# The low part of a mixer's weight: a negated copy on ScalarE and an adding transfer instead of a subtraction

## The chip, the core and the metric

The kernel runs on one core of a Trainium2 chip. The core has a matrix engine (TensorE, "PE" in the profile, its weight loads "PEld"), a vector engine (VectorE, "DVE"), an engine for activations and scaled copies (ScalarE, "ACT"), a general engine (GpSimd, "POOL") and SyncE ("SP"), which here issues transfers. Each engine has one queue of instructions and works it off in order; semaphores hold an instruction until what it needs is done. Sixteen DMA engines carry the transfers. The metric is the time of one execution in microseconds on the device; the median of several is what counts.

## What is computed

Two layers of a diffusion backbone work on 256 context and 256 latent tokens of 1024 channels. A layer normalises the tokens, multiplies them by one wide weight `w_in`, gives the products to three token mixers and a gate, merges the branches, and then runs a gated MLP:

```python
u_a, u_b, u_c, u_g = split_cols(h @ p['w_in'], [A_COLS, B_COLS, C_COLS, G_COLS])
...
y_a, y_ac = rwkv7_branch(u_a, u_ac, p)          # A: recurrence over the tokens, both directions
y_b, y_bc = rglru_branch(u_b, u_bc, p)          # B: gated linear recurrence
y_c, y_cc = na_branch(u_c, u_cc, p, update_ctx) # C: neighbourhood attention
x = x + g1 * rms_norm(merge_branches(u_g, y_a, y_b, y_c, p), ng[1])
h = rms_norm(x, ng[2]) * (1.0 + sc2) + sh2
x = x + g2 * rms_norm(conv_ffn(h, p), ng[3])
```

`w_in` has 11520 columns, 90 tiles of 1024 x 128 in each of the two layers. After the last layer only the latent tokens are wanted, so in the second layer gates, queries and some others are computed for 256 columns instead of 512.

## The kernel before

All large products run in float32r, a form of float32 to which a copy rounds. To keep the precision, each operand x is split into a high part hi (x rounded to float32r) and a low part lo = x - hi, and three products are summed: high weight by high tokens (line 246), high weight by low tokens (line 247), low weight by high tokens (line 248). A tile of a weight, 128 partitions by up to 1024 values, takes 8 times these three products.

`wload` (line 217) brings in one tile: SyncE issues the load of the raw tile `wr` (three places in the pool `wp`), ScalarE copies it into `wh` with rounding (line 225), and VectorE or GpSimd subtracts and writes `wl` (line 228). `wh` and `wl` have two places each in `wp`. So a tile's high and low part can be made when the products of the tile before last are done with theirs, while the tile before runs on TensorE. Which engine subtracts is read from the table `CFG[layer]['lo']`: a list for each phase of the layer, 0 for VectorE and 1 for GpSimd. The phases that matter here all load tiles of `w_in`: `st` (start of a layer), `1` (key, value and receptance of the next head pair), `X`, `Y` (recurrence B), `Q` (attention's query, key, value), `G` and `N` (gates). `proj` (line 252) is what they call.

The mixers go over eight head pairs. For a pair, the parts of mixer A's recurrence (line 720 the products r, 735 sa, 741 sp, each followed by an operation of ScalarE, VectorE or GpSimd on the state) alternate on TensorE with projections of B, C, the gates and the next pair. A triangular inverse of each pair's chunks runs on VectorE as some 30 pairs of short operations (lines 664 and 666). A scheduler sets the order on every engine when the kernel is built: it takes instructions by the priorities in `CFG` and by its own estimates of when each could start, so a change of one operation moves others. At run time the order is fixed.

Of the kernel before, what the change touches and what calls it, by code (L numbers as in the profile page):

```python
# [44 lines left out]
for _n, _c in _CS:  # L45
# [6 lines left out]
# per layer: the order in which a head pair's parts are traced, their priorities, how the products of the other  # L52
# mixers are spread beside them, and which engine takes the work that several could take
# [5 lines left out]
  'lo': {'1': [0, 0, 0],  # L59
         'G': [1],  # L60
         'N': [0],
         'Q': [0, 0, 0],
         'X': [0],
         'Y': [0],
# [5 lines left out]
         'st': [1],  # L70
# [38 lines left out]
  'lo': {'1': [0, 0, 0],  # L109
         'G': [1],  # L110
         'N': [0],
         'Q': [0, 1, 0],
         'X': [0],
         'Y': [1],
# [5 lines left out]
         'st': [0],  # L120
# [37 lines left out]
class Net:  # L158
# [51 lines left out]
    # ---- weights: raw -> (hi, lo) in float32r  # L210
    def phase(self, l, name, wps=None):
        """From here on the weights rotate among wps; where their low parts are worked out: 1 for GpSimd."""
        self.lo, self.wn = CFG[l]["lo"][name], 0
        if wps:
            self.wps, self.wi = wps, 0

    def wload(self, ap, kt):
# [8 lines left out]
        eng = nc.gpsimd if self.lo[self.wn % len(self.lo)] else nc.vector  # L226
        self.wn += 1
        eng.tensor_tensor(lo, raw, hi.bitcast(F32), op=ALU.subtract)  # L228
# [36 lines left out]
    # ---- rms statistics of the tokens a ... b - 1: acc holds the sums of squares over the channel tiles  # L265
# [15 lines left out]
    def stat(self, st, sq, a, b, first, last):  # L281
        """Adds the sums of sq over its channels to st, a column for 128 tokens."""
# [13 lines left out]
    # ---- conditioning vectors of a layer: mod[128, 48, 2]  # L296
# [16 lines left out]
    def ada_chunk(self, l, n, kind="c"):  # L313
        """Columns 512 n ... 512 n + 511 of the modulation, four column groups side by side on TensorE."""
# [22 lines left out]
        # modulation: h = x rstd (ng (1 + sc)) + sh ; x += (g ng) o rstd  # L337
# [12 lines left out]
    def layer_consts(self, l):  # L350
# [19 lines left out]
        # softplus(-lam) = max(-lam, 0) + log1p(exp(-|lam|)); log1p(u) = 2 atanh(u / (2 + u))  # L370
# [53 lines left out]
    # ---- A: RWKV-7  # L424
# [16 lines left out]
    def rw_start(self, Q):  # L441
# [4 lines left out]
        # stacked over the partitions: (hi, lo) of w, (lo, hi) of a  # L446
# [14 lines left out]
    def rw_key(self, R, Q, p, n0):  # L461
# [15 lines left out]
        # normalised key  # L477
# [93 lines left out]
    def rw_gram(self, R, u, n0):  # L571
        nc = self.nc
        KR, BK = u["KR"], u["BK"]
        G = R.tile([P, 2, 2, 2, NCH, 64], F32, tag="Gm", name="Gm")  # part, d, h, c
# [22 lines left out]
    def rw_rows(self, R, u, n0):  # L597
# [3 lines left out]
        # from here on [beta; k] decayed to the end of its chunk  # L601
# [3 lines left out]
        # value rows by token, for both directions  # L605
# [12 lines left out]
        # rows by token of [beta; k]  # L618
# [13 lines left out]
    def rw_inv(self, R, u):  # L632
# [9 lines left out]
        if self.cfg['f1']:  # L642
            # the block beside them makes room for the rows of keys
# [10 lines left out]
        # columns s of the inverse: rows 0-63 hold the odd ones, rows 64-127 the even ones, both in the even places  # L654
# [16 lines left out]
    def rw_inv2(self, R, u):  # L671
# [4 lines left out]
        T1 = Ap  # rows 0-31: T11, rows 96-127: Q  # L676
# [134 lines left out]
    # ---- B: RG-LRU  # L811
# [16 lines left out]
    def lru_gates(self, B, u, d):  # L828
# [4 lines left out]
        if self.cfg['lq']:  # L833
            # the parts of the products lie where the second direction's values come
# [54 lines left out]
    # ---- C: neighbourhood attention  # L889
    def softmax(self, C, ps, nk):  # L890
        """ps: list of PSUM views [128, nk] (same width); returns normalised probabilities in SBUF."""
# [22 lines left out]
    def attn_qkv(self, C, p, n0):  # L914
# [13 lines left out]
        # values: 4 windows of 4 rows by 32 columns, then the context  # L928
# [8 lines left out]
    def attn_pre(self, C, u, n0):  # L937
        nc = self.nc
        q, k, vw = u["q"], u["k"], u["vw"]
        # queries by blocks (n, r, c): rotated, then plain  # L940
# [8 lines left out]
        if self.cfg['sq']:  # L949
            # (hi, lo) of a head's plain queries over the partitions, the high parts in the head's own half; the  # L950
            # high parts of the context's keys in both halves, the low ones beside each other
# [489 lines left out]


class _Off:
    """Columns n0 ... 511 of the 512 tokens, addressed by their place among the 512."""

    def __init__(self, ap, n0):
        self.ap, self.n0 = ap, n0
# [147 lines left out]
```

## Time and profile before

| what | value |
|---|---|
| median of three runs | 3066.45 us |
| the three runs | 3055.29, 3066.45, 3069.74 us |
| span of the profiled execution, first to last instruction | 3050.6 us |
| TensorE busy in the span | 2886.2 us |
| VectorE busy | 1968.9 us |
| ScalarE busy | 1411.1 us |
| GpSimd busy | 840.6 us |
| mean granted clock of TensorE | 0.959 |

The profile's own execution is known by its span alone, which lies 16 us under the median of the runs and 5 us under the fastest; sums below are differences to that span and are then put on the median. The mixers of the first layer lie between about 30 and 1100 us, those of the second between 1790 and 2692 us; merging, output product and MLP fill the rest. A product's busy time is longer than the distance to the next one's start, as products are pipelined; distances between starts are the better price of a product.

### The profile page before, as it was taken

To read this page: it belongs to the slowest core of one execution; us is meant where nothing else is said; L and a number is where in the kernel's file an instruction comes from. 1 tells how busy PE (TensorE), PEld (TensorE's weight loads), DVE (VectorE), ACT (ScalarE), POOL (GpSimd) and SP (SyncE) were. 2 spreads that over 40 slices of the span, in tenths; PEclk is the share of its full clock that TensorE was granted. 3 is DMA by queue.
4 is the path that set the end of the run, shared out by engine and by line. 5 is a ranking of instruction groups with operands and counts; after the bars stand their busy time and mean duration, and the time that the engine had idled before them with its cause. 6 is when DMAs were issued, how large, how long until landed. Compare 5 with 4: busy or idle time off the path is not lost. (4 is left out here: it accounts for less than half of the span.)

```text
span 3050.6 us, 53179 instructions
## 1 busy us (share of the span) xinstructions
PE 2886.2 (95%) x21104; PEld 2265.9 (74%) x21104; DVE 1968.9 (65%) x3745; ACT 1411.1 (46%) x2485; POOL 840.6 (28%) x788
## 2 busy tenths in 40 slices
PE   7999999999999999999999998998999999998998
PEld 5666776766767678687778886776776777788898
DVE  6757658576686653465444267788677778775784
ACT  4454455554455452253323245454554545554553
POOL 3341322424234225100000113433432433414220
PEclk9999999999999899998999998998988999999899
DMA  6222122211222225755562352222222122245653
GB/s 229 81 70 67 59 71 66 74 60 56 69 76 70 84 100 180 273 190 180 198 223 92 107 183 82 62 78 69 68 72 69 62 70 78 77 140 205 222 188 115
DMA packets 130553, 344.39 MB, mean 113 GB/s; under 512 B 14720, under 2 KB 41600, under 8 KB 130304
## 3 DMA queue, kind: packets, MB, share of 16 engines
q1 hardware_dynamic: 123392, 334.69, 33.1%
q10 hardware_dynamic: 6912, 6.29, 0.7%
q8 instruction: 166, 2.72, 0.4%
q14 instruction: 83, 0.68, 0.1%
HBM read 301.08 MB, written 25.17 MB: 107 GB/s over the span
## 5 line engine op out<-in xcount | busy, mean ns | idle before, releaser
L225 ACT ACTIVATE wh<-wr 128x1024 fp32r<-128x1024 f32 (+1 forms) x402 | 420.8, 1048 | 581.0 <-PE pj L247 209.1
L248 PE MATMUL pj<-hh,wl 128*128 128x512 f32 (+1 forms) x1440 | 559.0, 389 | 41.4 <-DVE wl L228 40.0
L246 PE MATMUL pj<-hh,wh 128*128 128x512 f32 (+1 forms) x1440 | 569.7, 397 | 5.8 <-ACT gt L1088 3.0
L228 DVE TENSOR_TENSOR wl<-wr,wh 128x1024 fp32r<-128x1024 f32 (+1 forms) x310 | 398.2, 1285 | 266.5 <-ACT wh L225 244.2
L247 PE MATMUL pj<-hl,wh 128*128 128x512 f32 (+1 forms) x1440 | 556.0, 386 | 0.0
L228 POOL TENSOR_TENSOR wl<-wr,wh 128x1024 fp32r<-128x1024 f32 (+1 forms) x92 | 221.1, 2403 | 637.1 <-ACT wh L225 343.6
L248 PEld LDWEIGHTS pj<-hh,wl 128*128 128x128 f32 x1440 | 280.7, 195 | 104.6 <-DVE wl L228 45.7
L246 PEld LDWEIGHTS pj<-hh,wh 128*128 128x128 f32 x1440 | 280.6, 195 | 70.0 <-issue 16.4
L247 PEld LDWEIGHTS pj<-hl,wh 128*128 128x128 f32 x1440 | 280.4, 195 | 55.1 <-issue 13.4
L666 DVE TENSOR_TENSOR AT<-AT,itmp 128x126 f32<-128x126 f32 (+22 forms) x496 | 154.7, 312 | 11.8
L732 POOL TENSOR_TENSOR r<-SV,gC 64x256 f32<-64x256 f32 x96 | 84.2, 877 | 242.0 <-DVE SV L745 139.8
L664 DVE TENSOR_TENSOR itmp<-AT 128x126 f32<-128x126 f32 (+22 forms) x496 | 138.1, 278 | 12.0
L585 PEld LDWEIGHTS gram<-KR,BK 64*128 64x128 f32 x1024 | 116.3, 193 | 27.4 <-ACT Gm L590 14.8
L585 PE MATMUL gram<-KR,BK 64*128 64x128 f32 (+1 forms) x1024 | 131.3, 288 | 4.9 <-ACT Gm L590 4.7
L246 PE MATMUL fo<-fh,wh 128*128 128x256 f32 (+1 forms) x418 | 131.0, 313 | 0.0
L248 PE MATMUL fo<-fh,wl 128*128 128x256 f32 (+1 forms) x418 | 130.7, 313 | 0.0
L247 PE MATMUL fo<-fl,wh 128*128 128x256 f32 (+1 forms) x418 | 130.4, 312 | 0.0
L246 PE MATMUL fu<-hh,wh 128*128 128x256 f32 (+1 forms) x384 | 126.2, 330 | 3.1 <-DVE fgs L1347 2.4
L246 PE MATMUL fg<-hh,wh 128*128 128x256 f32 (+1 forms) x384 | 127.2, 333 | 0.1
L248 PE MATMUL fu<-hh,wl 128*128 128x256 f32 (+1 forms) x384 | 126.4, 330 | 0.8 <-DVE wl L228 0.8
L247 PE MATMUL fg<-hl,wh 128*128 128x256 f32 (+1 forms) x384 | 126.0, 330 | 0.0
L247 PE MATMUL fu<-hl,wh 128*128 128x256 f32 (+1 forms) x384 | 125.8, 328 | 0.0
(344 smaller groups left out, 6481.6 us busy)
## 6 DMA issues: line engine op xcount, KB each, us to landing
wr<-in_w_in SPq DMA_DIRECT2D x180, 512.0 KB, 3.2
aw<-in_ada_w SPq DMA_DIRECT2D x96, 512.0 KB, 4.4
wr<-in_ffn_w_in SPq DMA_DIRECT2D x96, 512.0 KB, 3.4
wr<-in_w_branch SPq DMA_DIRECT2D x48, 512.0 KB, 3.3
wr<-in_ffn_w_out SPq DMA_DIRECT2D x36, 512.0 KB, 3.5
wr<-in_w_out SPq DMA_DIRECT2D x24, 512.0 KB, 4.4
Gm<-KR SPq DMA_DIRECT2D x32, 256.0 KB, 3.6
wr<-in_ffn_w_out SPq DMA_DIRECT2D x18, 384.0 KB, 3.1
```

What stands on the lines that cost most here:

```text
L225: nc.scalar.activation(hi, raw, AF.Copy)
L228: eng.tensor_tensor(lo, raw, hi.bitcast(F32), op=ALU.subtract)
L246: nc.tensor.matmul(o, lhsT=a, rhs=xh[k][:, n0:n1], start=(first and k == 0), stop=False)
L247: nc.tensor.matmul(o, lhsT=a, rhs=xl[k][:, n0:n1], start=False, stop=False)
L248: m = nc.tensor.matmul(o, lhsT=b, rhs=xh[k][:, n0:n1], start=False, stop=(last and k == kt - 1))
L585: nc.tensor.matmul(ps[:, i, 0:nx], lhsT=BK[hs, d, c, :], rhs=KR[hs, 0:nx, d, c, :], start=True, stop=True)
L664: eng.tensor_tensor(tmp, Ap[:, q + 1:32, q:q + 1].to_broadcast([P, nt, ns]), Tf[:, q:q + 1, 0:2 * ns:2].to_broadcast([P, nt, ns]), op=ALU. ...
L666: eng.tensor_tensor(Tf[:, q + 1:32, 0:2 * ns:2], Tf[:, q + 1:32, 0:2 * ns:2], tmp, op=ALU.subtract)
L732: nc.gpsimd.tensor_tensor(sg, S0, gcb, op=ALU.mult)
```

## The change

In the phases `st`, `1`, `X`, `Y`, `Q`, `G` and `N` of both layers the table now holds 2. For these tiles no engine subtracts. ScalarE reads the raw tile a second time and writes it, rounded as the high part is, with the opposite sign into the low part's place; then GpSimd issues a transfer that reads the whole weight from DRAM once more and adds it to what stands there, so that x - hi remains. The tables of the other phases (`m0`, `m1`, `wo`, `fi`, `fo`, `fp`) stay, and the table of the second layer changes like the first's. Comments are dropped elsewhere in the file, and line numbers behind the edit grow by 5.

```diff
-  'lo': {'1': [0, 0, 0],
-         'G': [1],
-         'N': [0],
-         'Q': [0, 0, 0],
-         'X': [0],
-         'Y': [0],
+  'lo': {'1': [2],
+         'G': [2],
+         'N': [2],
+         'Q': [2],
+         'X': [2],
+         'Y': [2],
...
-         'st': [1],
+         'st': [2],
...
         nc.scalar.activation(hi, raw, AF.Copy)
-        eng = nc.gpsimd if self.lo[self.wn % len(self.lo)] else nc.vector
+        how = self.lo[self.wn % len(self.lo)]
         self.wn += 1
-        eng.tensor_tensor(lo, raw, hi.bitcast(F32), op=ALU.subtract)
+        if how == 2:
+
+            nc.scalar.activation(lo, raw, AF.Copy, scale=-1.0)
+            nc.gpsimd.dma_start(lo, ap, accum_op=ALU.add)
+        else:
+            (nc.gpsimd if how else nc.vector).tensor_tensor(lo, raw, hi.bitcast(F32), op=ALU.subtract)
```

The scheduler's order moves with it. 174 of the 402 tiles take the new way; VectorE has 177 subtractions of weights instead of 310, GpSimd 51 instead of 92, ScalarE 174 copies more, and GpSimd 174 transfers where it had none.

On TensorE, in the second layer where the key tile of a head pair (`pj11`) begins, the order before was this (`pj60` is the tile before, `lr` and `li` belong to mixer B, `pj36` is a tile of 256 columns, `wl_19601` and `wl_19730` are low parts):

```order
L248 MATMUL pj60_19597<-hh7_15574,wl_19601 128x512
L846 MATMUL lr_19633<-xb_19394,gw_19361 128x512
L847 MATMUL li_19634<-xb_19394,gw_19361 128x512
L246 MATMUL pj36_19646<-hh0_15567,wh_19649 128x256
L246 MATMUL pj11_19726<-hh0_15567,wh_19729 128x512
L247 MATMUL pj11_19726<-hl0_15575,wh_19729 128x512
L248 MATMUL pj11_19726<-hh0_15567,wl_19730 128x512
L246 MATMUL pj11_19726<-hh1_15568,wh_19729 128x512
```

And the same place in the changed kernel (`pj36` now stands as a whole between `pj60` and `pj11`, whose low part is `wl_19852`; `avt` are transposes of attention's values):

```order
L251 MATMUL pj36_19767<-hh7_15664,wh_19770 128x256
L252 MATMUL pj36_19767<-hl7_15672,wh_19770 128x256
L253 MATMUL pj36_19767<-hh7_15664,wl_19771 128x256
L987 MATMUL avt_19828<-cst_86,vw_19650 128x128 x4
L251 MATMUL pj11_19848<-hh0_15657,wh_19851 128x512
L252 MATMUL pj11_19848<-hl0_15665,wh_19851 128x512
L251 MATMUL pj19_19884<-hh0_15657,wh_19887 128x512
L253 MATMUL pj11_19848<-hh0_15657,wl_19852 128x512
```

The key tile's low part takes the place that `pj60` had; between the last product of `pj60` and the first low product of `pj11` there stand now the 24 products of `pj36`, four transposes and three products.

On VectorE, near the end of the inverse (`AT`, `itmp`) of that head pair, before:

```order
L664 TENSOR_TENSOR itmp_19342<-AT_19260 128x78
L666 TENSOR_TENSOR AT_19260<-AT_19260,itmp_19342 128x6x13
L664 TENSOR_TENSOR itmp_19345<-AT_19260 128x70
L666 TENSOR_TENSOR AT_19260<-AT_19260,itmp_19345 128x5x14
L228 TENSOR_TENSOR wl_19730<-wr_19727,wh_19729 128x1024
L664 TENSOR_TENSOR itmp_19348<-AT_19260 128x56
L666 TENSOR_TENSOR AT_19260<-AT_19260,itmp_19348 128x4x14
```

and in the changed kernel (`ib` and `z` belong to mixer B):

```order
L669 TENSOR_TENSOR itmp_19458<-AT_19376 128x78
L671 TENSOR_TENSOR AT_19376<-AT_19376,itmp_19458 128x6x13
L669 TENSOR_TENSOR itmp_19461<-AT_19376 128x70
L876 TENSOR_TENSOR ib_19518<-ib_19518,z_19517 128x1024
L671 TENSOR_TENSOR AT_19376<-AT_19376,itmp_19461 128x5x14
L878 SCALAR_TENSOR_TENSOR z_19517<-av_19516,ib_19518 128x512
L669 TENSOR_TENSOR itmp_19464<-AT_19376 128x56
```

The subtraction is gone from between the steps of the inverse, and operations of mixer B have moved in.

On GpSimd, at the same key tile, in the changed kernel (`bias` is attention's position bias, `z` and `sq` belong to mixer B):

```order
L975 TENSOR_TENSOR sw_19817<-sw_19817,cst2_16721 128x256
L231 DMA wl_19721<-in_w_in 128x1024
L231 DMA wl_19771<-in_w_in 128x1024
L924 TENSOR_TENSOR bias_19645<-bias_19645,cst2_16721 128x512
L231 DMA wl_19852<-in_w_in 128x1024
L884 TENSOR_TENSOR z_19517<-z_19517 128x256
L231 DMA wl_19888<-in_w_in 128x1024
```

Each transfer stands in line with the engine's other work, behind `bias` and in front of `z`, and waits there for ScalarE's copy.

## Rows read from the trace of the kernel before

**Rows 1.** The page's first part: busy us, share of the span, instructions of each engine.
```profile
PE 2886.2 (95%) x21104; PEld 2265.9 (74%) x21104; DVE 1968.9 (65%) x3745; ACT 1411.1 (46%) x2485; POOL 840.6 (28%) x788
```

**Rows 2.** Table by stretch, both mixers: engines' busy us (instructions), granted clock, DMA share, GB/s.
```profile
30.00:1100.00 1070.00, 1031.24 (x7204) 738.95 (x7197) 712.45 (x1504) 518.12 (x960) 345.98 (x342) 0.97 0.22 72
1790.00:2692.00 902.00, 840.65 (x6452) 653.03 (x6451) 690.56 (x1345) 466.76 (x841) 323.77 (x339) 0.94 0.24 78
```

**Rows 3.** List of waits, whole span: us in total, times, longest us.
```profile
DVE SV L745 <- PE sp L741: 115.1, 61, 4.5
...
PEld pj L248 <- DVE wl L228: 45.7, 15, 7.8
...
PEld r L720 <- DVE SV L745: 20.7, 26, 2.4
...
PEld sp L741 <- ACT SV L737: 17.1, 45, 0.8
...
PEld gram L585 <- ACT Gm L590: 14.8, 25, 1.9
...
PEld Q L685 <- DVE AT L678: 11.3, 10, 1.8
PEld sa L735 <- ACT r L724: 11.3, 38, 0.8
...
PEld yt L791 <- DVE cen L778: 9.9, 6, 3.2
...
PEld kbc L493 <- ACT th L490: 9.0, 8, 1.9
```

**Rows 4.** Line 228 in the second layer's mixers: who waited for it (us, times).
```profile
  PEld pj L248: 45.7, 15
```

**Rows 5.** Timeline at one such wait: start us, us, engine, work, idle before it.
```profile
2122.57 0.23 DVE L666 TENSOR_TENSOR AT<-AT,itmp 128x70 f32<-128x70 f32 x1
2122.72 1.22 DVE L228 TENSOR_TENSOR wl<-wr,wh 128x1024 fp32r<-128x1024 f32 x1
...
2123.99 0.29 PEld L248 LDWEIGHTS pj<-hh,wl 128*128 128x128 f32 x1 [7.81 <-DVE wl L228]
```

**Rows 6.** Table by stretch behind that wait (columns as in rows 2).
```profile
2124.00:2128.00 4.00, 4.00 (x9) 3.13 (x10) 3.72 (x11) 0.00 (x0) 0.00 (x0) 0.50 0.38 135
```

**Rows 7.** Timeline of TensorE, projections at full clock: starts of following products.
```profile
2237.23 0.39 PE L246 MATMUL pj<-hh,wh 128*128 128x512 f32 x1
2237.45 0.39 PE L247 MATMUL pj<-hl,wh 128*128 128x512 f32 x1
...
2238.02 0.28 PE L248 MATMUL pj<-hh,wl 128*128 128x256 f32 x1
2238.14 0.28 PE L246 MATMUL pj<-hh,wh 128*128 128x256 f32 x1
```

**Rows 8.** The page's groups: count, busy us, mean ns of one, idle before it.
```profile
L225 ACT ACTIVATE wh<-wr 128x1024 fp32r<-128x1024 f32 (+1 forms) x402 | 420.8, 1048 | 581.0 <-PE pj L247 209.1
...
L228 DVE TENSOR_TENSOR wl<-wr,wh 128x1024 fp32r<-128x1024 f32 (+1 forms) x310 | 398.2, 1285 | 266.5 <-ACT wh L225 244.2
...
L228 POOL TENSOR_TENSOR wl<-wr,wh 128x1024 fp32r<-128x1024 f32 (+1 forms) x92 | 221.1, 2403 | 637.1 <-ACT wh L225 343.6
...
L732 POOL TENSOR_TENSOR r<-SV,gC 64x256 f32<-64x256 f32 x96 | 84.2, 877 | 242.0 <-DVE SV L745 139.8
```

**Rows 9.** Timeline: a subtraction on GpSimd, a step of the inverse on VectorE.
```profile
2111.09 2.44 POOL L228 TENSOR_TENSOR wl<-wr,wh 128x1024 fp32r<-128x1024 f32 x1
...
2111.30 2.38 DVE L666 TENSOR_TENSOR AT<-AT,itmp 128x126 f32<-128x126 f32 x1
```

**Rows 10.** The page's DMA parts: a queue's share; an issue's size and us to landing.
```profile
q1 hardware_dynamic: 123392, 334.69, 33.1%
...
wr<-in_w_in SPq DMA_DIRECT2D x180, 512.0 KB, 3.2
```

**Rows 11.** Timeline of SyncE: one issue of a transfer.
```profile
327.65 0.33 SPq L1089 DMA_DIRECT2D gd<-gt  x1
```

More of the change, by code (lines that the diff above doesn't have):

```diff
@@ L108 @@
   'hp': 10000,
[L109 to L114, printed above, removed]
+  'lo': {'1': [2],
+         'G': [2],
+         'N': [2],
+         'Q': [2],
+         'X': [2],
+         'Y': [2],
          'fi': [0, 1, 0],
@@ L119 @@
          'm1': [0],
-         'st': [0],
+         'st': [2],
          'wo': [1]},
```

## The prediction

> **What bounds the kernel now.** I read the page first for the engines' shares: TensorE is busy for 2886 us of a span of 3050.6, 95% [rows 1]. So whatever happens elsewhere counts only where TensorE waits. Then I read the two mixer stretches, which hold all the weights that the change touches: in the first layer TensorE is busy for 1031 of 1070 us, in the second for 841 of 902, while VectorE is at 67% and 77% and ScalarE at 48% and 52% [rows 2]. The list of waits then says what TensorE idles for there. The largest single entry is a projection's third product (line 248) that waits for its weight's low part from VectorE: 45.7 us in 15 waits on the weight-load side [rows 3]. All 45.7 us lie in the second layer's mixers [rows 4].
>
> The timeline shows what one of them is. A product's weight load stands idle for 7.81 us until 2123.99, and VectorE does the subtraction of 1.22 us at 2122.72, behind a long row of steps of 0.2 to 0.3 us of a triangular inverse [rows 5]. VectorE was not short of time for the subtraction, the subtraction stood late in its queue. And TensorE pays again afterwards: the granted clock of the 4 us behind that wait is 0.50, the lower of its two levels [rows 6], which loses another 2 us.
>
> **What the change removes.** 174 of the 402 weights change their way. The order of instructions on VectorE loses 133 subtractions and GpSimd's loses 41. At 1.285 and 2.403 us each [rows 8] that is 171 us of VectorE and 99 us of GpSimd. TensorE sees of it the 45.7 us above: the inverse no longer stands in front of a low part. The other waits of TensorE for VectorE in the list sum to 20.7 + 11.3 + 9.9 = 42 us [rows 3]. VectorE's busy share in the mixers falls from 71% (1403 of 1972 us, [rows 2]) to 62%, so I take an eighth of the 42 off, 5 us; half of it, 21 us, is the most I would believe. GpSimd's subtractions also held VectorE up: a step of the inverse took 2.38 us beside one of them [rows 9], where others take 0.23 [rows 5]. That is VectorE's time off the path and I leave it at nothing.
>
> **What it adds, outside the new chain.** ScalarE gets 174 more copies of the high part's form, 1.048 us each [rows 8]: 182 us, so its share in the mixers goes from 50% to 59%. TensorE's waits for ScalarE in the recurrence and beside it are 17.1 + 11.3 + 14.8 + 9.0 = 52 us [rows 3]; scaled by 59/50 they cost 10 us more. The second reading of 174 weights is 91 MB. At the rate of the load queue (334.69 MB in 33.1% of 3050.6 us, or 331 GB/s, [rows 10]) one takes 1.6 us of all sixteen DMA engines, whose mean share in the mixers is 0.22 to 0.24 [rows 2]: one reading adds 0.14 to that share, two passes 0.28. There is room; cost nothing. The raw tile has three places, so holding it for one more copy costs nothing either; what hides that is that loads are issued a tile ahead.
>
> **The new chain, and what it does to TensorE.** A low part has two places. The place is free when the last low product of the tile before last is done. From then on the changed kernel needs, in a row: the semaphore, 0.1 us; ScalarE's high part, 1.05; the instructions that stand on ScalarE between high and low part, 1.9 on the mean in the new order, at 0.55 each (985 us in 1801 instructions, [rows 2]), 1.1; the negated copy, 1.05; GpSimd's queue, 0.4 (a third of the time busy, with instructions of 0.98 us on the mean, [rows 2]); the issue of the transfer; and its landing. The trace has no transfer issued by GpSimd and none that adds. For the issue the ends are 0.33 us (an issue of SyncE, [rows 11]) and 2.4 (the subtraction that it replaces there, [rows 8]); I take 1.0, nearer to the first, since no data passes through the engine. For the landing the ends are a plain load of the same 512 KB, 3.2 us, and two of them one behind the other, 6.4 [rows 10]; the add must read the destination as well as the weight, so neither end fits, and I take the middle, 4.8. Sum: 0.1 + 1.05 + 1.1 + 1.05 + 0.4 + 1.0 + 4.8 = 9.5 us, against about 2.4 for the two operations of before.
>
> How long may it be? I counted, in the changed kernel's order on TensorE, the work between that release and the first low product of the new tile, each product at the mean distance from start to start that its form has in the trace (at full clock 0.23 us for 512 columns, 0.12 for 256, [rows 7]; the means are longer, as they hold before's waits and its slow clock). For 172 tiles the median span is 12.2 us. 14 spans are under 7 us, 25 under 8, 47 under 9, 59 under 9.5, 72 under 11, 86 under 12. The tight ones are the key tiles of the next head pair, 5 to 7 us in both layers, and in the second layer the 256-column tiles and those behind them. What is missing, summed over the tiles, is 19 us for a chain of 7 us, 38 for 8, 69 for 9, 96 for 9.5, 126 for 10, 192 for 11, 271 for 12. As a check, the same count in the order of before gives 31 us for a chain of 5 and 51 for 6, where the trace has 45.7: so before's chain acted as one of 5.7 us, 3.3 more than its two operations, and the excess was the queue. With that excess instead of my 1.5 us of queues the new chain would be 11.3 us and miss some 215 us; I keep it for the range, as ScalarE and GpSimd have no row of waiting work like VectorE's inverse.
>
> What is queued behind the new waits: on ScalarE the copies of the recurrence, on GpSimd the scaled state of line 732 (96 of them, 0.88 us, [rows 8]), which the next step of the recurrence adds. VectorE takes that only after another product, for which it already waits 115 us [rows 3], so a delay of a microsecond there is covered; a longer one is not.
>
> The load row alone would make the landing 3.2 us, the chain 7.9 and the sum of the next part 3,061 us. The Trainium skill, page Collectives: The Full Stack, section "Why ReduceScatter is half of AllGather", says that an add inside the DMA engines needs two reads for each write and so runs at half the copy's rate; by it, the 1.6 us of moving double and the landing is an estimate of 4.8 us, which gives 3,121. No run here has yet shown which.
>
> **The sum.** +96 (missing in the chain) - 46 (the old wait) + 10 (ScalarE) - 5 (VectorE) = +55 us. The loss of clock behind each wait is on both sides, about 2 us each time, and I let it cancel. On the profiled execution that is a span of 3050.6 + 55 = 3,106 us. The median of the three runs is 3066.45, 16 us above that span (the runs lie between 3055.29 and 3069.74), so the forecast is 3066 + 55 = **3,121 us**.
>
> **Rivals.**
> *The old wait goes and nothing takes its place* (faster). The scheduler has put the tiles further apart than before, and if the chain takes no more than 7 us only 19 us are missing. Time: 3066 + 19 - 46 - 21 = 3,018 us. For it speaks that only 14 spans are under 7 us; against it, that even a plain load leaves 7.9 us by the rows. It decides from a chain below 7.5 us (27 us missing). Chance 0.26, between 2,995 and 3,050.
> *A draw.* The chain is about 8 us, 38 us missing: 3066 + 38 - 46 + 5 = 3,063 us. Chance 0.16.
> *The add is slow or the issue is* (much slower). A landing of 6.4 and an issue of 2.4 make the chain 12.5 us: some 317 us missing, 3066 + 317 - 46 + 5 = 3,342 us. Every second tile would then stop TensorE, evenly in both layers. Chance 0.12 for 3,250 and more.
> *The recurrence pays* (slower). 128 state copies of 0.38 us on ScalarE (line 737) and 96 operations of line 732 on GpSimd now have 174 copies and as many waiting issues between them. If each of the 96 comes a microsecond later than VectorE asks for it, that is 96 us in place of the count above, 3066 + 96 - 46 + 5 = 3,121 us: the forecast's time by another road, with VectorE and not a DMA named behind TensorE's waits. Chance 0.12.
> That the change doesn't do what it says is excluded by the order: 174 transfers on GpSimd, 174 copies on ScalarE, no subtraction of these tiles left.
>
> **How the numbers follow.** Forecast, from 3,082 to 3,250, chance 0.34 by the DMA chain and 0.12 by the recurrence; draw 0.16; faster 0.26; much slower 0.12. A measurement of this kernel can tell about 0.5% from no change, 15 us. Faster 0.26, same 0.16, slower 0.58. The range leaves some tenth out at either end: from 3,025, inside the fast rival, to 3,270, just inside the slow one.
>
> **What would show it.** In the changed kernel's list of waits, "wl from VectorE" should be gone for projections, and in its place a wait of line 253's products for a DMA, some 60 to 120 us in 40 to 70 pieces, longest at the key tiles, in both layers. The DMA part should list 174 transfers of 512 KB at 4 to 6 us to landing. VectorE should fall by about 170 us, ScalarE rise by 180, TensorE's busy time stay. A landing under 3.5 us would make the fast rival true; one above 6 the slow one. If there is no wait for a DMA and the time is still longer, the recurrence's waits on lines 725, 740 and 746 must have grown, and the count of spans was beside the point.

## The result, and the profile after

The changed kernel takes 3312.16 us, the median of four runs (3305.81 to 3319.99), beside 3060.87 us for the kernel before on the same chip (3052.03 to 3069.74). The ratio is 1.0819, 95% interval 1.0782 to 1.0856. The forecast was 3121 us with a range up to 3270: the direction was right and the size was not.

The page's first part, which answers to [rows 1]; the span of this execution is 3306.2 us, that of before 3050.6:

```profile
PE 3008.7 (91%) x21104; PEld 2356.1 (71%) x21104; DVE 1765.3 (53%) x3612; ACT 1571.4 (48%) x2659; POOL 844.8 (26%) x921
```

TensorE does the same 21104 products, but is busy 122.5 us longer and idle for 297.5 us where it was 164.4. These two, 122.5 and 133.1, are the whole 255.6 us of longer span. The table by stretch for the mixers, which answers to [rows 2], shows where the busy time came from. The stretches are cut a little inside the mixers: the last recurrence product `sp` of the first layer now starts at 1217.6 where it was 1092.5, 125 us later, and the second layer's projections now run from 1935 to 2954.

```profile
30.00:1170.00 1140.00, 1028.52 (x6630) 739.89 (x6625) 603.55 (x1384) 564.62 (x991) 346.80 (x396) 0.89 0.43 101
1900.00:2900.00 1000.00, 898.08 (x6429) 700.64 (x6427) 570.23 (x1272) 537.48 (x920) 306.25 (x394) 0.88 0.48 114
```

The granted clock was 0.97 and 0.94 there, and is 0.89 and 0.88. The DMA engines' share doubled, from 0.22 and 0.24 to 0.43 and 0.48. The list of waits (us in total, times, longest), to set beside [rows 3], names what TensorE idles for, and the last two lines who releases the two transfers of a tile:

```profile
PEld pj L253 <- DMA wl<-in_w_in: 191.3, 67, 6.8
PE pj L253 <- DMA wl<-in_w_in: 169.0, 61, 6.1
...
PEld sp L746 <- ACT SV L742: 20.1, 49, 1.0
PEld r L725 <- DVE SV L750: 16.6, 40, 0.8
...
PEld sa L740 <- ACT r L729: 13.7, 44, 0.6
...
PEld gram L590 <- ACT Gm L595: 8.7, 16, 1.2
PEld Q L690 <- DVE AT L683: 7.6, 8, 1.8
...
POOL wl L231 <- ACT wl L230: 495.3, 105, 22.4
...
SPq L222 <- ACT wl L230: 908.7, 128, 17.9
```

The old wait for a subtraction is gone. In its place the same product (now line 253) waits 191.3 us in 67 pieces for the adding transfer. On the side of the products the wait is 169.0 us, where the kernel before had this line:

```profile
PE pj L248 <- DVE wl L228: 40.0, 9, 7.4
```

The 129.0 us between the two are nearly all of the 133.1 us by which TensorE's idle time grew. The other waits of TensorE are near what they were. Groups and DMA issues of the page, to set beside [rows 8] and [rows 10] (group: count, busy us, mean ns; queue: packets, MB, share of 16 engines; issue: count, KB, median us to landing):

```profile
L231 POOL DMA_DIRECT2D wl<-in_w_in x174 | 154.1, 886 | 622.8 <-ACT wl L230 495.3
L233 DVE TENSOR_TENSOR wl<-wr,wh 128x1024 fp32r<-128x1024 f32 (+1 forms) x177 | 226.8, 1282 | 176.6 <-ACT wh L225 175.5
...
q1 hardware_dynamic: 123392, 334.69, 32.2%
q0 software_dynamic: 25056, 91.24, 16.1%
...
wr<-in_w_in SPq DMA_DIRECT2D x180, 512.0 KB, 3.8
wl<-in_w_in POOLq DMA_DIRECT2D x174, 512.0 KB, 7.8
```

The issue on GpSimd takes 0.89 us, and the landing 7.8 us from the start of the issue. The timeline of one tile shows why the two releases belong together: ScalarE's negated copy ends at 331.23, and releases two transfers at once, the raw load of a later tile at 331.26 and this tile's adding transfer at 331.53.

```profile
330.19 1.04 ACT L230 ACTIVATE wl<-wr 128x1024 fp32r<-128x1024 f32 x1
...
331.26 0.33 SPq L222 DMA_DIRECT2D wr<-in_w_in  x1
...
331.53 0.86 POOL L231 DMA_DIRECT2D wl<-in_w_in  x1 [8.06 <-ACT wl L230]
...
339.51 0.19 PEld L253 LDWEIGHTS pj<-hh,wl 128*128 128x128 f32 x1 [3.23 <-DMA wl<-in_w_in]
```

The table by stretch in and behind this wait (columns as in rows 2) shows the DMA engines at a share of 0.64 while TensorE waits, where the whole stretch has 0.43, and then at nothing. It has 11 products in 4 us at a clock of 0.57, mostly the lower of the two levels, 1.2 GHz, and 27 in the next 3.5 us at 1.00, which is 2.4 GHz:

```profile
335.60:339.50 3.90, 0.83 (x11) 0.54 (x10) 1.73 (x3) 3.64 (x5) 0.93 (x1) 1.00 0.64 151
339.50:343.50 4.00, 3.98 (x11) 3.12 (x12) 4.00 (x4) 0.00 (x0) 3.42 (x2) 0.57 0.00 0
343.50:347.00 3.50, 3.50 (x27) 2.71 (x25) 1.43 (x2) 0.82 (x1) 1.42 (x2) 1.00 0.00 0
```

### The profile page after: what moved, and what is told of

Same layout as the page of the kernel before. It is cut to its first block, busy times and chain, and to the rows that moved or that the text cites. A ratio compares the mean times of both kernels' runs of the same rounds, so it can differ in the third digit from the quotient of the medians.

```text
span 3306.2 us, 53463 instructions
## 1 busy us (share of the span) xinstructions
PE 3008.7 (91%) x21104; PEld 2356.1 (71%) x21104; DVE 1765.3 (53%) x3612; ACT 1571.4 (48%) x2659; POOL 844.8 (26%) x921
## 3 DMA queue, kind: packets, MB, share of 16 engines
q0 software_dynamic: 25056, 91.24, 16.1%
## 5 line engine op out<-in xcount | busy, mean ns | idle before, releaser
L253 PE MATMUL pj<-hh,wl 128*128 128x512 f32 (+1 forms) x1440 | 596.4, 415 | 169.5 <-DMA wl<-in_w_in 169.0
L251 PE MATMUL pj<-hh,wh 128*128 128x512 f32 (+1 forms) x1440 | 592.9, 413 | 12.0 <-ACT gt L1093 5.9
L252 PE MATMUL pj<-hl,wh 128*128 128x512 f32 (+1 forms) x1440 | 586.1, 407 | 0.0
L253 PEld LDWEIGHTS pj<-hh,wl 128*128 128x128 f32 x1440 | 299.8, 208 | 247.1 <-DMA wl<-in_w_in 191.3
L251 PEld LDWEIGHTS pj<-hh,wh 128*128 128x128 f32 x1440 | 302.2, 210 | 78.7 <-issue 19.4
L233 DVE TENSOR_TENSOR wl<-wr,wh 128x1024 fp32r<-128x1024 f32 (+1 forms) x177 | 226.8, 1282 | 176.6 <-ACT wh L225 175.5
L231 POOL DMA_DIRECT2D wl<-in_w_in x174 | 154.1, 886 | 622.8 <-ACT wl L230 495.3
L233 POOL TENSOR_TENSOR wl<-wr,wh 128x1024 fp32r<-128x1024 f32 (+1 forms) x51 | 121.4, 2380 | 511.7 <-DVE fgs L1352 287.8
L230 ACT ACTIVATE wl<-wr 128x1024 fp32r<-128x1024 f32 x174 | 182.9, 1051 | 0.4 <-PE pj L253 0.2
L750 DVE TENSOR_TENSOR SV<-sp,r 64x256 f32<-64x256 f32 x96 | 39.8, 415 | 227.6 <-PE sp L746 226.4
L671 DVE TENSOR_TENSOR AT<-AT,itmp 128x126 f32<-128x126 f32 (+22 forms) x496 | 132.4, 267 | 12.8
L729 ACT ACTIVATE r<-r 64x256 f32<-64x256 f32 x128 | 48.6, 380 | 179.5 <-PE r L725 165.0
```

Of the source, the lines that this page charges most:

```text
L230: nc.scalar.activation(lo, raw, AF.Copy, scale=-1.0)
L231: nc.gpsimd.dma_start(lo, ap, accum_op=ALU.add)
L233: (nc.gpsimd if how else nc.vector).tensor_tensor(lo, raw, hi.bitcast(F32), op=ALU.subtract)
L251: nc.tensor.matmul(o, lhsT=a, rhs=xh[k][:, n0:n1], start=(first and k == 0), stop=False)
L252: nc.tensor.matmul(o, lhsT=a, rhs=xl[k][:, n0:n1], start=False, stop=False)
L253: m = nc.tensor.matmul(o, lhsT=b, rhs=xh[k][:, n0:n1], start=False, stop=(last and k == kt - 1))
```

## The experiments

Times are medians; the ratio is to the kernel before, run on the same chip in the same job.

**1. The same transfer without the add.** The order of instructions on all five engines is that of the changed kernel.

```diff
-            nc.gpsimd.dma_start(lo, ap, accum_op=ALU.add)
+            nc.gpsimd.dma_start(lo, ap)
```

> The changed kernel with one thing taken out: GpSimd's transfer writes the weight over the negated copy instead of adding it (so the low part is the whole weight and the result is not the reference's). The order on all five engines is that of the changed kernel. Landing theory (the slowdown is the adding transfer's 7.8 us against two places for low parts, and the half clock behind each wait): without the second read the landing falls by some 1.5 us to about 6.2, TensorE's waits for it from 191 to 100 to 140 us, the time to 3,160 to 3,230 us. Order theory (the slowdown comes from the new order and from the longer queues on ScalarE and GpSimd, whatever the transfer takes): 3,290 us or more.

Measured: 3104.49 us, ratio 1.017 (1.0129 to 1.0211). The page and the list of waits of this run:

```profile
L231 POOL DMA_DIRECT2D wl<-in_w_in x174 | 101.4, 583 | 543.2 <-ACT wl L230 416.6
...
q0 software_dynamic: 25056, 91.24, 8.7%
...
wl<-in_w_in POOLq DMA_DIRECT2D x174, 512.0 KB, 4.5
```

```profile
PEld pj L253 <- DMA wl<-in_w_in: 63.3, 42, 3.9
```

With a landing of 4.5 us in place of 7.8, the excess over the kernel before falls from 251 to 51 us, further than expected. The new order of instructions and the copies and issues in the queues are still there, and cost 51 us at most, so the theory that blamed the order falls. The add doubles the transfers' engine time: 16.1% of 3306.2 us against 8.7% of 3102.8, 532 against 270 us for the same bytes.

**2. Three places for low parts**, paid for with a raw place. This is meant to take the wait for a free place off the chain and to leave the transfer as it is.

```diff
-        raw = pool.tile([P, 1024], F32, tag="wr", name="wr", bufs=3 if pool is self.wp else None)[:, :kt * P]
+        raw = pool.tile([P, 1024], F32, tag="wr", name="wr", bufs=2 if pool is self.wp else None)[:, :kt * P]
...
-        lo = pool.tile([P, 1024], F32R, tag="wl", name="wl")[:, :kt * P]
+        lo = pool.tile([P, 1024], F32R, tag="wl", name="wl", bufs=3 if pool is self.wp else None)[:, :kt * P]
...
-        lw = self.wp.tile([P, 1024], F32, tag="wr", name="lw", bufs=3)[:, :640]
+        lw = self.wp.tile([P, 1024], F32, tag="wr", name="lw", bufs=2)[:, :640]
```

> The changed kernel with three places for low parts instead of two in the weights' pool, paid for with two places for raw weights instead of three. Landing theory: a third place gives each low part one more tile's time, so waits for the transfer fall under 60 us, the granted clock comes back to 0.94 or more, and the time is 3,040 to 3,110 us. Order theory: the same copies and transfers stand in the queues, so 3,230 us or more.

Measured: 3064.4 us, ratio 1.0028 (1.0007 to 1.0048). Nearly everything is regained; 11 us are left. Its list of waits and its DMA part held a surprise:

```profile
PEld pj L253 <- DMA wl<-in_w_in: 49.2, 14, 5.7
...
SPq L222 <- ACT wh L225: 609.0, 114, 16.6
```

```profile
q0 software_dynamic: 25056, 91.24, 17.4%
...
wl<-in_w_in POOLq DMA_DIRECT2D x174, 512.0 KB, 5.5
```

The landing itself fell to 5.5 us, while the transfers' engine time stayed: 17.4% of 3063.9 us are 533 us, where the changed kernel had 532. So in the changed kernel the adding transfer does not take more of the engines, it is spread over a longer time.

With a free place at hand the scheduler puts the negated copy ahead of the high part's in 156 of 174 tiles, and the raw load is then released by the high copy (line 225) and no longer by the negated one. I went through all 174 adding transfers of both traces, and call one accompanied when a raw load is issued between 1 us before and 1.5 us after it. In the changed kernel 145 are, and land after 7.9 us (median). Here 26 are, and land after 7.5, while the 69 with no raw load from 3 us before to 4 us after land after 5.3. The order on ScalarE goes with it within this one run: of the 156 tiles with the negated copy first 10 are accompanied, and the 156 land after 5.4; of the other 18, 16 are, and the 18 land after 7.7. So the landing seems to depend on company; experiment 9 tests this.

The rule is rough: in the changed kernel the 29 that are not accompanied still land after 6.9, nearly all of them beside some other transfer; only 3 of the 174 share no more than 1 us with any, and these land after 5.3 to 5.5.

**3. One layer at a time.** The table of one layer is set back to that of before, so that only the other layer uses the transfer.

> The new way in the first layer's mixers alone, the second layer as before. Landing theory: 92 us of waits and as much again in clock are new there, and before had no wait of this kind to lose: 3,061 plus 120 to 160, so 3,180 to 3,220 us. Order theory: half of the slowdown, about 3,185 us, with waits spread over other lines and no fall of the clock.

> The new way in the second layer's mixers alone, the first layer as before. Landing theory: 93 us of new waits less the 46 us of old ones, and the clock: 3,061 plus 80 to 130, so 3,140 to 3,190 us, and this and the first-layer kernel's excess together make the whole 251 us. Order theory: the same sum, but no smaller than the first layer's half.

Measured: 3188.75 us, ratio 1.0441 (1.0396 to 1.0486), for the first layer alone and 3170.51, ratio 1.0387 (1.0327 to 1.0447), for the second. The excesses of 135 and 117 us sum to 252, the whole. The loss lies in both layers and they do not share it.

**4. The negated copy first.**

```diff
+            nc.scalar.activation(lo, raw, AF.Copy, scale=-1.0)
+            nc.gpsimd.dma_start(lo, ap, accum_op=ALU.add)
             nc.scalar.activation(hi, raw, AF.Copy)
-            nc.scalar.activation(lo, raw, AF.Copy, scale=-1.0)
-            nc.gpsimd.dma_start(lo, ap, accum_op=ALU.add)
```

> The changed kernel with ScalarE's two copies of a weight tile in the other order: the negated copy first and the adding transfer issued behind it, the high part after that. One copy (1.05 us) leaves the chain from a free place to a landed low part, and the adding transfer begins before ScalarE has released the raw tile's place, so its start no longer coincides with the load of a later raw tile. If the waits come from the length of this chain, 1.0 to 2.0 us less of it takes 80 us for each us (the counted spans between a chain of 11 and of 12 us), half as much again for the clock: 3130 to 3240 us, the landing down from 7.8 to 6.0 to 7.5 us. If instead the high part was what TensorE needed first and the delay moves to it, PEld's and PE's waits for the high copy on ScalarE grow by 100 us or more in all and the time stays at 3280 us or above.

Measured: 3245.15 us, ratio 1.0622 (1.0575 to 1.067), just outside the expected 3130 to 3240. The excess over the kernel before falls from 251 to 195 us, but the landing stayed at 7.5 us, and 142 adding transfers are still accompanied by a raw load. The edit did only a part of what it says: in the trace the negated copy runs ahead of the high one in 51 of the 174 tiles, and in the other 123 the scheduler still puts the high copy first. The 51 land after 7.0 us, the 123 after 7.8. So the run does not price a chain without the high copy, and whether a shorter chain and a landing without company come together it leaves open.

**5. The low products last**, in the changed kernel and in the kernel before.

```diff
         for k in range(kt):
-            a, b = hi[:, k * P:(k + 1) * P], lo[:, k * P:(k + 1) * P]
+            a = hi[:, k * P:(k + 1) * P]
             nc.tensor.matmul(o, lhsT=a, rhs=xh[k][:, n0:n1], start=(first and k == 0), stop=False)
-            nc.tensor.matmul(o, lhsT=a, rhs=xl[k][:, n0:n1], start=False, stop=False)
-            m = nc.tensor.matmul(o, lhsT=b, rhs=xh[k][:, n0:n1], start=False, stop=(last and k == kt - 1))
+            m = nc.tensor.matmul(o, lhsT=a, rhs=xl[k][:, n0:n1], start=False, stop=False)
...
+        for k in range(kt):
+            m = nc.tensor.matmul(o, lhsT=lo[:, k * P:(k + 1) * P], rhs=xh[k][:, n0:n1], start=False, stop=(last and k == kt - 1))
```

> The changed kernel with the products of a weight tile in another order: all products with the high part first, then those with the low part (same products, same sum). The low part of a full tile is wanted 14 to 16 products of 0.23 us later, some 3.5 us, while its place comes free as late as before. If the length of the chain against the span between two uses of a place is the cause, this is a chain of 9 us in place of 12.5: 70 to 130 us of waits in place of 360, less lost clock: 3060 to 3140 us. If the waits come from somewhere else (the transfers' total, GpSimd's queue), no wait is shortened and the time stays above 3250 us.

> The kernel before with the same order of products (all with the high part, then all with the low one), subtraction as it was. If the kernel before lost its 46 us of waits for the low part, and the half-clock stretches behind them, to a part that came 1 to 3 us late, these go: 2990 to 3035 us. If the waits for the attention and recurrence operands set the time there, or move into the place of the old ones, 3040 to 3070 us.

Measured: 3146.77 us, ratio 1.0296 (1.0243 to 1.035), with the transfer, and 3195.9, ratio 1.0429 (1.0356 to 1.0503), with the subtraction. The first fits the theory of the span between uses, a little above the expected range: the landing is still 7.7 us, and TensorE's waits for it fall from 191.3 to 85.7 us, with the granted clock at 0.940:

```profile
PEld pj L256 <- DMA wl<-in_w_in: 85.7, 44, 4.4
```

The second was a plain miss. No wait of a projection for its low part is left in its list, and yet the kernel loses 4%. The profile is of the longest of its four executions, 3222.18 us; the other three had a mean granted clock of 0.919 to 0.932, where the kernel before in the same job had 0.952 to 0.964. Their span times the missing clock is 215 to 259 us, where the kernel before had 110 to 147, so most of the loss goes with the lower clock. What lowers the clock there, without those waits, I did not find.

**6. Control: the kernel before with the places of experiment 2.**

> Control for the run of the changed kernel with three places for low parts and two for raw tiles: the kernel before with the same places, subtraction as it was. If the third place is worth as much to the kernel before (its waits of 46 us were for a place that came free late), 3000 to 3035 us. If its waits were for VectorE's queue behind other work, the place takes nothing off, and two raw places cost it some: 3045 to 3090 us.

Measured: 3092.01 us, ratio 1.014 (1.0085 to 1.0196). The two changes of places together cost the subtraction 1.4%, although its waits for low parts fall from 45.7 to 28.7 us; which of the two costs it, this run does not show. With equal places the adding transfer is the faster way, by 1.1%.

```profile
PEld pj L253 <- DVE wl L233: 28.7, 12, 5.1
```

**7. A better third place.** In experiment 2 the second layer's key tiles still waited 3.0 to 3.6 us each on the side of the products. The timeline of one shows a raw place held by the recurrence's small weights (`lw`, loaded at 2122.64): VectorE's last reading of them (line 241) ends at 2128.61, the next raw load follows at 2128.68, and the wait for the low part ends at 2140.13.

```profile
2122.64 0.33 SPq L470 DMA_DIRECT2D lw<-in_lora  x1
...
2125.53 0.63 ACT L238 ACTIVATE lh<-lw 128x512 fp32r<-128x512 f32 x1 [1.97 <-DMA lw<-in_lora]
...
2127.92 0.69 DVE L241 TENSOR_TENSOR ll<-lw,lh 128x512 fp32r<-128x512 f32 x1
...
2128.68 0.33 SPq L222 DMA_DIRECT2D wr<-in_w_in  x1
...
2132.07 1.06 ACT L230 ACTIVATE wl<-wr 128x1024 fp32r<-128x1024 f32 x1 [4.37 <-DMA wr<-in_w_in]
...
2140.13 0.29 PEld L253 LDWEIGHTS pj<-hh,wl 128*128 128x128 f32 x1 [3.82 <-DMA wl<-in_w_in]
```

So the small weights got another place, on top of experiment 2; the second run adds the edit of experiment 4, the third is the subtraction with the same places.

```diff
-        lw = self.wp.tile([P, 1024], F32, tag="wr", name="lw", bufs=2)[:, :640]
-        nc.sync.dma_start(lw, self.ins["lora"][self.l, p])
+        lw = T2("ta")
+        nc.sync.dma_start(lw, self.ins["lora"][self.l, p, :, :512])
...
-        nc.gpsimd.tensor_copy(gw, lw[:, 512:])
+        nc.sync.dma_start(gw, self.ins["lora"][self.l, p, :, 512:])
```

> The changed kernel with three places for low parts and two for raw tiles, as in the run with three places, and with the recurrence's small weights (lora, 640 columns) no longer loaded into a raw place: 512 columns go to a scratch tile of the recurrence (ta), 128 straight into the gate's weights (gw). In the run with three places the second layer's key tiles still waited 3.0 to 3.6 us each, 24 us in all, and there the raw load of the key tile was issued only once the lora tile had left one of the two raw places. If that place was the cause, the 24 us and the half-clock stretches behind them go: 3020 to 3045 us. If two raw places are too few in themselves, or the scratch tile comes free too late, 3050 to 3080 us.

> As the run with the lora weights' own place, and with ScalarE's negated copy ahead of the high part's. The chain is one copy (1.05 us) shorter and the adding transfer starts before the raw place is released. If chain length still costs with three places, 10 to 30 us under that run: 3000 to 3030 us. If the third place has already covered the chain, the same time within 10 us.

> Control: the kernel before (subtraction) with the same places, three low, two raw, and the lora weights in the scratch tile. With three low and two raw places the subtraction ran at 1.014 and the adding transfer at 1.003 of the kernel before, some 30 us apart. If VectorE's and GpSimd's freed time is worth that wherever the landing is covered, this run is 20 to 40 us above the one with the transfer: 3045 to 3080 us. If those 30 us came from the lora tile in the raw places, the two meet within 10 us.

Measured: 3036.15 us, ratio 0.9916 (0.9886 to 0.9946); 3030.99, ratio 0.9899 (0.9872 to 0.9927); 3088.63, ratio 1.0082 (1.0055 to 1.0109). The first two beat both kernels, and can't be told from each other: in the first the scheduler already runs the negated copy ahead in 163 of 174 tiles, so the edit of experiment 4 changes only the other 11. The waits of the first and, in the second fence, of the subtraction with the same places:

```profile
PEld pj L253 <- DMA wl<-in_w_in: 20.5, 12, 6.5
```

```profile
PEld pj L253 <- DVE wl L233: 37.5, 9, 5.4
```

The transfer and the subtraction are now 52 us apart, in the transfer's favour. The waits for low parts differ by 17 us only; between the two profiled executions TensorE is also busy 46 us less, 2879.4 against 2925.7, and what brings that is not shown.

**8. The old wait by another road.** In the kernel before, one number of the table moves the second layer's key subtraction to GpSimd.

```diff
-  'lo': {'1': [0, 0, 0],
+  'lo': {'1': [1, 0, 0],
```

> The kernel before with one number changed: in the second layer the subtraction of the recurrence's key tile goes from VectorE to GpSimd. The 46 us of waits for the low part lay at these key tiles, 2.9 to 7.4 us each. If they were VectorE's queue, they shrink by half or more though GpSimd takes 2.4 us in place of 1.3: 3020 to 3045 us. If the high part itself came late, or GpSimd is behind its own work there, 3045 to 3075 us.

Measured: 3090.39 us, ratio 1.01 (1.0074 to 1.0127), above both expected ranges. TensorE's waits for low parts fall from 45.7 to 19.4 us (10.7 for GpSimd, 8.7 for VectorE), more than the half that was to speak for VectorE's queue. But another wait, 11.3 us in [rows 3], grows by 46.6 us:

```profile
PEld Q L690 <- DVE AT L683: 57.9, 14, 8.1
...
PEld pj L253 <- POOL wl L233: 10.7, 9, 1.9
...
PEld pj L253 <- DVE wl L233: 8.7, 5, 5.2
```

**9. The raw load cut to an eighth.** Seven eighths of the raw load are left out; ScalarE's two copies, whose edits are not shown, read the 128 columns that are left eight times over, so that the high parts hold repeated values.

```diff
-        nc.sync.dma_start(raw, ap)
+        small = self.lo[0] == 2; nc.sync.dma_start(raw[:, :P] if small else raw, ap[:, :P] if small else ap)
...
```

> The changed kernel with the mixers' raw tile loads cut to 128 of their 1024 columns (64 KB in place of 512 KB; ScalarE's two copies read these columns eight times over). It leaves out seven eighths of the raw load, so the high parts hold repeated values; copies, adding transfers, products and places are as in the changed kernel. In the changed kernel 172 of 174 adding transfers lay over 2 us or more of another transfer, mostly the raw load that the same negated copy releases, and landed after 7.8 us; the few without landed after 5.3 to 5.5. If this sharing is what made 7.8 of them, the landing falls to 5.2 to 5.8 us, the chain to 10 us, and the time to 3130 to 3210 us, near the kernel's counted 126 us of waits plus clock. If 7.8 us is the adding transfer's own time at this place (its reads of the low part, its packets), the landing stays above 7 us and the time above 3270 us.

Measured: 3126.76 us, ratio 1.0202 (1.0145 to 1.026). DMA part and waits:

```profile
wl<-in_w_in POOLq DMA_DIRECT2D x174, 512.0 KB, 5.5
wr<-in_w_in SPq DMA_DIRECT2D x174, 64.0 KB, 1.9
```

```profile
PE pj L253 <- DMA wl<-in_w_in: 77.4, 39, 5.1
PEld pj L253 <- DMA wl<-in_w_in: 54.6, 35, 4.7
```

147 adding transfers are still accompanied, by a raw load of 64 KB now, and land after 5.5 us. It was the sharing that made 7.8 us of it. The time is a little below the expected range, 71 us above the kernel before in the same job. The waits, 77.4 us in 39 pieces on the side of the products and 54.6 in 35 on that of the weight loads, lie about the lower end of the forecast's 60 to 120 us in 40 to 70 pieces. The landing is the firmer reading of the two, since the order is not quite that of the changed kernel: on GpSimd 172 of 921 positions hold another instruction.

## Why the prediction was wrong

**The landing was the mis-sized term.** I took 4.8 us, between one plain load and two, as if the transfer had the engines to itself, and 1.0 us for the issue beside it. The profile counts a landing from the start of its issue, so my bounds of 3.2 and 6.4 us held an issue already, and the 7.8 us measured stand against the two terms together, 5.8. By itself the adding transfer lands after 5.3 us, issue included (experiment 2). It is hardly ever by itself in the changed kernel: I wrote that holding the raw tile for one more copy costs nothing, and did not ask what that copy's end releases besides the adding transfer. It releases the next raw load too, and the two share the sixteen engines for 7.8 us. "There is room" was read from the mean DMA share of 0.22 to 0.24 [rows 2], an average over microseconds in which nothing moves. With seven eighths of the raw load gone the kernel is 71 us above the kernel before (experiment 9), where the forecast had 55.

The Trainium skill, page Collectives: The Full Stack, section "Why ReduceScatter is half of AllGather", has the add of a collective, done in the DMA engines, run at half the copy's rate because it reads twice for each write. The runs agree: 532 against 270 us of engine time. The price that the prediction drew from it for a transfer alone, an estimate of 4.8 us, is near the 5.3 measured; the 2.5 us on top come only in company. For those the Trainium skill has a rule that I had not weighed, page DMA: Bandwidth & Descriptors, section "Issuing engines are not separate DMA queues": transfers issued by different engines end up on the same sixteen DMA engines and interleave. Experiment 9 agrees, with 5.5 against 7.8 us, and so does the engine time of the adding transfers, the same 532 and 533 us at either landing.

**The clock did not cancel.** I put about 2 us of lost clock behind each wait on both sides of the sum, and expected TensorE's busy time to stay. But the waits for low parts went from 15 to 67, and the loss went with them:

| kernel | landing, us | PEld waits for low parts, us | granted clock | span x (1 - clock), us | TensorE busy, us |
|---|---|---|---|---|---|
| before | – | 45.7 | 0.959 | 125 | 2886.2 |
| changed | 7.8 | 191.3 | 0.912 | 291 | 3008.7 |
| negated copy first | 7.5 | 174.9 | 0.922 | 253 | 2977.8 |
| first layer only | 7.7 | 140.0 | 0.937 | 200 | 2936.9 |
| second layer only | 7.9 | 98.2 | 0.942 | 183 | 2937.8 |
| low products last | 7.7 | 85.7 | 0.940 | 189 | 2935.3 |
| without the add | 4.5 | 63.3 | 0.943 | 177 | 2918.2 |
| small raw load | 5.5 | 54.6 | 0.945 | 172 | 2907.2 |
| three places | 5.5 | 49.2 | 0.949 | 156 | 2900.5 |
| own place for small weights | 5.7 | 20.5 | 0.957 | 130 | 2879.4 |

(The row of the first layer alone holds 46.1 us of waits for the second layer's subtractions.) In the kernels with the transfer the fifth column grows with the third nearly throughout. It does not for the subtraction: its three variants with places or engine changed (experiments 6, 7 and 8) have waits of 28.7, 37.5 and 19.4 us and lose 148, 158 and 148, and the one of experiment 5 has no such waits in its list and a clock of 0.919 to 0.932. So other things lower the clock too. Of TensorE's 46 idle gaps of 2.5 us or more in the changed kernel, 42 have a stretch at half clock that begins in them or shortly behind them; the kernel before has 13 such gaps, 11 of them so. That idling causes the half clock is argued from this; no run changed the one without the other. Of the 255.6 us of longer span, 122.5 are products that ran slower, a term my sum did not have.

**The count of spans held roughly.** With the landing counted from the start of the issue, and no issue beside it, a landing of 4.5 us makes a chain of 8.2 us, for which the count gives about 44 us; the trace has 63.3. A landing of 7.8 us makes a chain of 11.5, about 231 us by the count, and the trace has 191.3. The rival of the slow add came near the measured 3312 us with its 3342, and was partly lucky: its sum holds 276 us more of idle time and nothing for the clock, where the trace has 133.1 more idle and 122.5 of slower products. Its mechanism was half right: a slow landing, but not a slow issue (0.89 us where it had 2.4), and a shared one.

**What was right.** The old wait of 45.7 us is gone. The subtractions on VectorE fell from 398.2 to 226.8 us, the forecast 171 (VectorE as a whole fell by 204; the other 32 I did not trace). The issue took 0.89 us, the forecast 1.0. The waits lie in both layers. The term of 10 us for TensorE's waits for ScalarE did not come: sp, sa and gram are together 42.5 us in place of 43.2, and the fourth, 9.0 us at line 493, is gone. ScalarE rose by 160 us, the forecast 180. The recurrence did not pay, and the draw and the faster case needed a chain of 8 us or less. The forecast named a landing above 6 us as the sign of the slow rival, and that sign came true.

## What to carry to other kernels

Before pricing a transfer, ask what the event that releases it releases as well: two transfers let go by one copy share the engines just then, however low their mean share is. A longer way to an operand needs one more place for it; this change cost 8% with two places, came out almost even with three, and gained 1% with three and another place for the small weights. A change of such a kind should be judged with the places it needs. The order of lines in the source is not the order on an engine: before reading an experiment on order, count in the trace how many tiles it moved. And where waits are multiplied, price the lost clock behind each of them instead of letting it cancel; in the changed kernel TensorE's longer busy time, 122.5 us, was about as large as its longer idle time.

## What the runs showed of the hardware

An adding transfer of 512 KB from DRAM into SBUF landed 5.3 us after the start of its issue when no raw load was issued near it (experiment 2), and after 7.9 us beside one of the same size (the changed kernel); the plain one took 4.5 us from GpSimd, mostly in that company (experiment 1). The adding transfers took 532 us of the sixteen engines, the plain ones 270. The issue on GpSimd took 886 ns with the add and 583 without. That a third place also shortened the landing, along with a change of ScalarE's order and so of the moment at which the raw load is released, I had not expected. What remains open is what lowers the clock when the low products come last in the kernel before, and whether idling alone does so in the changed one.
